# FoX attention and RWKV-7 in one stream of matmuls: transposes and logits set at other distances

## The chip, the core and the metric

One core of a Trainium2 chip runs the kernel in one launch. TensorE (PE in the profile) does the matmuls, VectorE (DVE), ScalarE (ACT) and GpSimd (POOL) the elementwise work, SyncE (SP) issues most transfers. The metric is the time of one execution on the device in microseconds (us), the median of several runs.

## The reference

A decoder layer in fp32 on 512 tokens of width 2048. One input projection feeds two mixers with 16 heads of 64 each:

```
z = rmsnorm(x) @ w_in                     # RWKV columns, FoX columns, gates
RWKV-7, per head, token by token:
  S = S * w - (S kk) (kk a)^T + v k^T ;  y = S r      # then group norm, bonus, SiLU gate
FoX, per head, in blocks of 128 queries:
  logits = q k^T / 8 + c_q - c_k          # c: running sum of log forget gates; causal
  o = softmax(logits) v                   # then SiLU gate
merged = sigmoid(g1) * (y_rw @ w_up_rwkv) + sigmoid(g2) * (y_fox @ w_up_fox)
x = x + merged @ w_out ; x = x + (p @ ple_proj) * sigmoid(rmsnorm(x) @ ple_gate_w) ; rmsnorm
```

## The kernel before

Every large product is done as three matmuls of 128x512 (high times high, high times low, low times high part of an fp32 number; `step`, L157). ScalarE makes the high part `hi` and VectorE the low part `lo` of each weight slab (L155, L156), a few slabs ahead. The instructions of a product stand in the main stream of TensorE; a block of 16 steps, 48 matmuls, makes one 128x512 result.

The mixers work on pairs of heads. For each of eight pairs `p` the main stream does the RWKV products k, v, r, g (`rw_k` ...) and then the FoX products k, q, v, g (`fx_k` ...), and seven blocks of gate products follow the last pair. Beside it two generators run per pair, `rw_mixer` and `fox_mixer`. Each does a little work and then yields a number of nanoseconds: the time, counted by the model in `Tensor.t` from the start of that piece of work, before which it is not called again. `Streams.drive` takes a generator's next piece when its time has come and otherwise the next step of the main stream. So the order on TensorE is fixed when the program is built, by these numbers; at run time TensorE takes its instructions strictly in that order and waits where one isn't ready. The order on the other engines is the framework's, except where `keep` pins it.

`fox_mixer` goes over eight blocks of a pair, four per head. `decays` prepares the bias of a block on GpSimd (`dd`, two buffers). `weights` does the logits in two matmuls (`lg`), which VectorE reads while adding the bias (L753, tile `dd`, with the row minimum `nm`); ScalarE does the exponential and the scaling. Later the weights are transposed by TensorE (`pT`, one transpose per 128 columns), ScalarE copies them out (`pt`, L789), and `values` multiplies them with the values (`po`) one block later. `lg`, `pT` and the transposed values `fvt` all use one PSUM bank (tag `F`, one buffer, L705): each must wait until the one before has been read. Before the change a round is: `lg` of block b+1, 5200 ns, `pT` of block b, and `lg` of block b+2 1500 ns after that.

`rw_mixer` works in PSUM tiles of tag `A`, two buffers that all its tiles take in turn: among others `gb` and `gk` (products of the decayed keys; VectorE reads them at L542, L543, L562, L564), `bo` and `rv`, the inverse in `x3` and `x4`, `u` (which ScalarE copies into `bd`, L632), `tr`, `py`, and at the end the transposes `yt` of the pair before (read by ScalarE, L694). L552 and L565 are the two yields that the diff touches, ahead of `gk` and ahead of `bo` and `rv`.

Of the kernel before, what the change touches and what calls it, by code (L numbers as in the profile page):

```python
# [108 lines left out]
def build(tc, a, out, dbg=None):  # L109
# [300 lines left out]
    def psa(shape, name):  # L410
        return psx.tile(shape, F32, tag="A", bufs=2, name=name)
# [4 lines left out]
    def need(z, *names):  # L416
        while any(n not in z for n in names):
            yield 450

    def rw_mixer(p, z):  # L420
# [128 lines left out]
            dma.dma_start(ldr[i : i + 8].rearrange("c i t -> i c t"), lt[bs, :, 32 * b : 32 * b + 32])  # L549
        lr = b4([P, 32, 32], f"lr{p}")  # L550
        dma.dma_start(lr, ldr.unsqueeze(0).to_broadcast([4, 32, 32, 32]).rearrange("g q i t -> g q (i t)"))
        yield 3500  # L552
        both = []
        for q in range(2):
            ps = psa([P, 4, P], f"gk{p}_{q}")
# [3 lines left out]
        for q, ps in enumerate(both):  # L559
# [2 lines left out]
                v.tensor_tensor(lak[half(h), cs, half(h)], ps[half(h), :, 0:64],  # L562
                                smb(slice(0, 64), half(h)), op=ALU.mult)
            v.tensor_tensor(ka[:, cs, 0:64], ps[:, :, 64:128], smb(slice(64, 128), slice(0, P)), op=ALU.mult)  # L564
        yield 5000  # L565
        ps = psa([P, T], f"bo{p}")
        pe.matmul(ps, bonesr, rh, start=True, stop=False)
        pe.matmul(ps, bonesr, rl, start=False, stop=True)
# [131 lines left out]
    def f2(name, bufs=None):  # L700
        return big.tile([P, T], F32, tag="f2", bufs=F2, name=name)

    def psf(shape, name):
        return psx.tile(shape, F32, tag="F", bufs=1, name=name)

    def fox_mixer(p, z):
        vt = f2(f"fvt{p}").rearrange("p (j d) -> p j d", d=P)
        done = []

        def token_major():  # L710
            ps = psf([P, 4, P], f"fvt{p}")
            for j in range(4):
                pe.transpose(ps[:, j], z["v"][:, j * P : (j + 1) * P], ident)
            s.copy(vt, ps)
            done.append(1)

        yield from need(z, "k", "q")
        q, k = z["q"], z["k"]

        qs, ks = ([big.tile([P, T], F32R, tag="f2", bufs=F2, name=f"{n}{p}_{h}") for h in range(2)] for n in ("qs", "ks"))  # L720
        kl = [small["kl", h] for h in range(2)]
        for h in range(2):
            hs, ho = slice(64 * h, 64 * h + 64), slice(64 - 64 * h, 128 - 64 * h)
            s.copy(qs[h][hs], q[hs])
            v.tensor_tensor(qs[h][ho], q[hs], qs[h][hs].bitcast(F32), op=ALU.subtract)
            s.copy(ks[h][hs], k[hs])
            s.copy(ks[h][ho], k[hs])
            v.tensor_tensor(kl[h][hs], k[hs], ks[h][hs].bitcast(F32), op=ALU.subtract)
            yield 1400
        o = f2(f"fo{p}")  # L730
        blocks = [(h, i) for h in range(2) for i in range(4)]
        cb, dds, pos = {}, {}, {}

        def fetch(h):
            cb[h] = big.tile([P, T], F32, tag="cb", bufs=1, name=f"cb{2 * p + h}")
            dma.dma_start(cb[h], cdr[2 * p + h : 2 * p + h + 1, :].to_broadcast([P, T]))

        def decays(h, i):

            hd, n = 2 * p + h, (i + 1) * P  # L740
            dd = dds[h, i] = big.tile([P, T], F32, tag="dd", bufs=2, name=f"dd{hd}_{i}")
            g.tensor_scalar(dd[:, :n], cb[h][:, :n], -1.0, cq[:, i, hd : hd + 1], op0=ALU.mult, op1=ALU.add)  # L742
            g.affine_select(out=dd[:, n - P : n], in_=dd[:, n - P : n], pattern=[[-1, P]], compare_op=ALU.is_ge,
                            fill=NEG, base=0, channel_multiplier=1)

        def weights(h, i):
            hd, n, dd = 2 * p + h, (i + 1) * P, dds[h, i]
            nm = big.tile([P, 2], F32, tag="nm", bufs=4, name=f"nm{hd}_{i}")
            lg = psf([P, T], f"lg{hd}_{i}")
            pe.matmul(lg[:, :n], qs[h][:, i * P : n], ks[h][:, 0:n], start=True, stop=False)  # L750
            pe.matmul(lg[:, :n], qs[h][:, i * P : n], kl[h][:, 0:n], start=False, stop=True)

            v.tensor_tensor_reduce(dd[:, :n], lg[:, :n], dd[:, :n], -1.0, 3.4e38, op0=ALU.add, op1=ALU.min,  # L753
                                   accum_out=nm[:, 0:1])
            s.activation(dd[:, :n], dd[:, :n], AF.Exp, scale=-1.0, bias=nm[:, 0:1], accum_out=nm[:, 1:2])  # L755
            v.reciprocal(nm[:, 1:2], nm[:, 1:2])
            s.activation(dd[:, :n], dd[:, :n], AF.Copy, scale=nm[:, 1:2])

        def values(h, i, pt):

            hs = slice(64 * h, 64 * h + 64)
            if i == 0:
                pos[h] = psx.tile([P, T], F32, tag="O", bufs=1, name=f"po{p}_{h}")
            for j in range(i + 1):
                pe.matmul(pos[h][:, i * P : (i + 1) * P], vt[:, j], pt[:, j], start=(j == 0), stop=(j == i))
            if i == 3:
                s.copy(o[hs], pos[h][hs])

        late = []

        fetch(0)
        yield 4000
        decays(0, 0)
        yield 1500
        weights(0, 0)
        for b, (h, i) in enumerate(blocks):
            if (h, i) == (0, 3):
                fetch(1)
                yield 4000
            if b < 7:  # L780
                decays(*blocks[b + 1])
                yield 1500
                weights(*blocks[b + 1])
            yield 5200 if b < 7 else 5500
            ps = psf([P, 4, P], f"pT{2 * p + h}_{i}")
            for j in range(i + 1):
                pe.transpose(ps[:, j], dds[h, i][:, j * P : (j + 1) * P], ident)
            pt = big.tile([P, 4, P], F32, tag="pt", bufs=2, name=f"pt{2 * p + h}_{i}")
            s.copy(pt[:, 0 : i + 1], ps[:, 0 : i + 1])  # L789
            if late:  # L790
                late.pop()()
            late.append(lambda h=h, i=i, pt=pt: values(h, i, pt))
            if not done:
                yield 2200
                yield from need(z, "v")
                yield 1500
                token_major()
                yield 1300
        yield 2600
        late.pop()()  # L800
        yield from need(z, "g")
        sg = f2(f"fsg{p}")
        s.activation(sg, z["g"], AF.Tanh)
        v.scalar_tensor_tensor(sg, sg, 1.0, z["g"], op0=ALU.add, op1=ALU.mult)
        y = f2(f"fy{p}")
        v.tensor_tensor(y, o, sg, op=ALU.mult)
        dma.dma_start(ydr_fx[p], y)
# [9 lines left out]
    def main():  # L817
# [15 lines left out]
        for p in range(NPAIR):  # L833
            z = {}
            streams.spawn(rw_mixer(p, z))
            for name, i in RW_ORDER:
                if (p, i) == (0, RW_ORDER[0][1]):
                    ps = small["ps_r"]
                else:
                    ps = psmain(f"rw{p}_{name}")  # L840
                    yield from product(ps, w_rw[p, i], xs)
                zt = b2(f"z{name}{p}")
                shifted(big, ps, 8 * i + p, zt)
                z[name] = zt
            z = {}
            streams.spawn(fox_mixer(p, z))
            for name, i in FX_ORDER:
                ps = psmain(f"fx{p}_{name}")
                yield from product(ps, w_fx[p, i], xs)
                zt = f2(f"fz{name}{p}")  # L850
                if name in "qg":
                    v.scalar_tensor_tensor(zt, ps, 0.125 if name == "q" else 0.5, rb, op0=ALU.mult, op1=ALU.mult)
                else:
                    v.tensor_tensor(zt, ps, rb, op=ALU.mult)
                z[name] = zt
# [283 lines left out]
```

## Time and profile before

| | |
|---|---|
| median of 3 runs | 1925.48 us (1923.34 to 1926.66) |
| the profiled execution | 1926.43 us, span 1924.7 us |
| TensorE busy in it | 1885.3 us, 98% of the span |
| VectorE, ScalarE, GpSimd busy | 1044.9, 853.3, 160.3 us |
| granted TensorE clock, mean | 0.994 of full speed |

The span goes from the first to the last instruction; 1.73 us of the execution lie outside it. The mixers run from about 40 to 1060 us, the gates and up-projections to 1535, the output projection to 1709, the rest to the end. A wait is shown at the instruction that waited, with the instruction that released it. A matmul's shown length includes its way through the array, so that matmuls overlap in the rows: the distance from start to start is what one costs.

### The profile page before, as it was taken

How to read it: one execution, taken by the hardware profiler on the slowest of the kernel's cores; microseconds unless marked ns; L12 is line 12 of the kernel's file. 1: busy time of each engine (PE TensorE's matmuls, PEld its weight loads, DVE VectorE, ACT ScalarE, POOL GpSimd, SP SyncE). 2: the span in 40 equal slices, each digit the busy share in tenths (PEclk: the TensorE clock that was granted, in tenths of full speed). 3: DMA queues.
4: the chain of work that ended last, by engine and by line, in shares of the span. 5: the costliest groups of instructions: out<-in, count | busy, mean ns of one | idle time of the engine just before them, and what ended most of it. 6: DMA issues, size and time to landing. Idle time of an engine off the chain costs nothing.

```text
span 1924.7 us, 26112 instructions
## 1 busy us (share of the span) xinstructions
PE 1885.3 (98%) x9722; PEld 1573.5 (82%) x9722; DVE 1044.9 (54%) x2255; ACT 853.3 (44%) x1608; POOL 160.3 (8%) x281
## 2 busy tenths in 40 slices
PE   8999999999999999999999999999999999999997
PEld 6878888888888888888888888888888888888887
DVE  7765756757567576675754433343333533434445
ACT  6536346364563644636446322232222433334333
POOL 1201102011020110201101000000000001101112
PEclk9999999999999999999999999999999999999998
DMA  5331322323222222232323533342233344463224
GB/s 169 94 93 64 107 80 86 95 72 99 88 78 100 76 96 88 74 102 64 106 89 98 181 115 110 99 140 92 97 99 99 99 142 141 155 207 99 96 95 161
DMA packets 87391, 204.31 MB, mean 106 GB/s; under 512 B 24784, under 2 KB 31184, under 8 KB 87264
## 3 DMA queue, kind: packets, MB, share of 16 engines
q1 hardware_dynamic: 85888, 201.39, 32.7%
q8 instruction: 76, 1.25, 0.3%
q10 hardware_dynamic: 1376, 1.25, 0.2%
q14 instruction: 51, 0.42, 0.1%
HBM read 186.06 MB, written 16.55 MB: 105 GB/s over the span
## 4 chain that ended last, share of the span: by engine, by line
PE 52%; ACT 1%; DVE 1%; issue 0%; POOL 0%; DVEq 0%
PE gate L63 18%; PE pg L63 9%; PE up L63 9%; PE wo L63 9%; PE pp L63 1%; PE rw_g L63 1%; PE fx_q L63 1%; PE fx_k L63 1%; PE py L63 0%; PE fx_g L63 0%; PE po L63 0%; PE rw_r L63 0%; PE lg L63 0%; ACT bd L632 0%; PE rw_v L63 0%
## 5 line engine op out<-in xcount | busy, mean ns | idle before, releaser
L155 ACT CAST hi<-raw 128x512 fp32r<-128x512 f32 x595 | 368.7, 621 | 796.9 <-PE gate L63 211.5
L156 DVE TENSOR_TENSOR lo<-raw,hi 128x512 fp32r<-128x512 f32 x596 | 412.8, 694 | 483.5 <-ACT hi L155 466.5
L63 PE MATMUL gate<-xh,hi 128*128 128x512 f32 x512 | 201.0, 393 | 0.0
L63 PE MATMUL gate<-xh,lo 128*128 128x512 f32 x512 | 199.6, 390 | 0.0
L63 PE MATMUL gate<-xl,hi 128*128 128x512 f32 x512 | 199.5, 390 | 0.0
L63 PEld LDWEIGHTS gate<-xh,lo 128*128 128x128 f32 x512 | 96.1, 188 | 20.1
L63 PEld LDWEIGHTS gate<-xh,hi 128*128 128x128 f32 x512 | 96.2, 188 | 19.3
L63 PEld LDWEIGHTS gate<-xl,hi 128*128 128x128 f32 x512 | 96.2, 188 | 19.3
L63 PE MATMUL pg<-x2h,hi 128*128 128x512 f32 (+1 forms) x304 | 109.0, 359 | 0.0
L63 PE MATMUL pg<-x2h,lo 128*128 128x512 f32 (+1 forms) x304 | 108.3, 356 | 0.0
L63 PE MATMUL pg<-x2l,hi 128*128 128x512 f32 (+1 forms) x304 | 108.2, 356 | 0.0
L742 POOL TENSOR_SCALAR dd<-cb,cq 128x128 f32<-128x128 f32 (+1 forms) x64 | 39.8, 622 | 663.0 <-PE pT L70 602.2
L595 DVE TENSOR_TENSOR nn<-nn,tp 128x240 f32<-128x240 f32 (+14 forms) x240 | 69.1, 288 | 7.3
L935 POOL TENSOR_TENSOR acc<-acc,sq 128x512 f32<-128x512 f32 x15 | 19.4, 1291 | 643.6 <-ACT sq L934 643.6
L591 DVE TENSOR_TENSOR tp<-nn,lr 128x240 f32<-128x240 f32 (+14 forms) x240 | 68.7, 286 | 5.9
L63 PEld LDWEIGHTS pg<-x2h,hi 128*128 128x128 f32 x304 | 57.5, 189 | 8.8 <-ACT hi L155 0.5
L63 PEld LDWEIGHTS pg<-x2h,lo 128*128 128x128 f32 x304 | 57.5, 189 | 8.5 <-DVE lo L156 0.4
L63 PEld LDWEIGHTS pg<-x2l,hi 128*128 128x128 f32 x304 | 57.5, 189 | 8.3 <-issue 0.2
L63 PE MATMUL rw_g<-xh,hi 128*128 128x512 f32 x128 | 53.5, 418 | 0.0
L63 PE MATMUL rw_r<-xh,hi 128*128 128x512 f32 x128 | 53.2, 415 | 0.0
L63 PE MATMUL rw_v<-xh,hi 128*128 128x512 f32 x128 | 53.0, 414 | 0.0
L755 ACT ACTIVATE dd<-dd,nm 128x128 f32<-128x128 f32 (+1 forms) x64 | 35.9, 562 | 37.4 <-DVE nm L753 36.9
(544 smaller groups left out, 4411.8 us busy)
## 6 DMA issues: line engine op xcount, KB each, us to landing
raw<-in_w_mix SPq DMA_DIRECT2D x126, 512.0 KB
raw<-in_w_gate SPq DMA_DIRECT2D x64, 512.0 KB
raw<-in_w_pg SPq DMA_DIRECT2D x36, 512.0 KB
raw<-in_w_out SPq DMA_DIRECT2D x32, 512.0 KB
raw<-in_w_up_rw SPq DMA_DIRECT2D x16, 512.0 KB
raw<-in_w_up_fox SPq DMA_DIRECT2D x16, 512.0 KB
x<-in_xT SPq DMA_DIRECT2D x16, 256.0 KB
cb<-cdr SPq DMA_DIRECT2D x16, 256.0 KB
```

Source lines behind the costliest of these rows:

```text
L63: self.eng.matmul(out, lhsT, rhs, start=start, stop=stop, skip_group_check=skip)
L155: (v.tensor_copy if made[0] == 0 else s.copy)(hi[:, :w], src)
L156: v.tensor_tensor(lo[:, :w], src, hi[:, :w].bitcast(F32), op=ALU.subtract)
L591: one = v.tensor_tensor(tp[:, :, 0:m], nn[:, :, j : j + 1].to_broadcast([P, 8, m]), lr[:, j : j + 1, j + 1 : 32].to_broadcast([P, 8, m]), ...
L595: v.tensor_tensor(nn[:, :, j + 1 : 32], nn[:, :, j + 1 : 32], tp[:, :, 0:m], op=ALU.add)
L742: g.tensor_scalar(dd[:, :n], cb[h][:, :n], -1.0, cq[:, i, hd : hd + 1], op0=ALU.mult, op1=ALU.add)
L755: s.activation(dd[:, :n], dd[:, :n], AF.Exp, scale=-1.0, bias=nm[:, 0:1], accum_out=nm[:, 1:2])
L935: g.tensor_tensor(acc, acc, sq, op=ALU.add)
```

## The change

In `fox_mixer` the yield of 5200 ns between the logits of block b+1 and the transposes of block b becomes 2600 ns, and 2600 ns are added between the transposes and the next piece (for all blocks; for block 0 in place of 2200 ns, and after the last block in place of the 2600 ns that stood behind the loop). After the logits of block 0 there are 4000 ns more before those of block 1. In `rw_mixer` the yield before `gk` grows from 3500 to 4400 ns, the one before `bo` and `rv` from 5000 to 6000 ns. No operation is added or removed; the moves are in the order of instructions.

```diff
@@ rw_mixer
-        yield 3500
+        yield 4400
         both = []
         for q in range(2):
             ps = psa([P, 4, P], f"gk{p}_{q}")
...
-        yield 5000
+        yield 6000
         ps = psa([P, T], f"bo{p}")
@@ fox_mixer
         weights(0, 0)
+        yield 4000
         for b, (h, i) in enumerate(blocks):
...
                 weights(*blocks[b + 1])
-            yield 5200 if b < 7 else 5500
+            yield 2600 if b < 7 else 5500
             ps = psf([P, 4, P], f"pT{2 * p + h}_{i}")
...
             late.append(lambda h=h, i=i, pt=pt: values(h, i, pt))
+            yield 2600
             if not done:
-                yield 2200
                 yield from need(z, "v")
                 yield 1500
                 token_major()
                 yield 1300
-        yield 2600
         late.pop()()
```

Three places show what becomes of it, each from TensorE's order. The first is the opening of pair 3 during its last FoX product `fx3_g`: `lg6_0` and `lg6_1` are the logits of blocks 0 and 1 of head 6, `pT6_0` the transpose of block 0. Before:

```order
L63 MATMUL lg6_0_4796<-ks3_0_4680,qs3_0_4678 128x128
L63 MATMUL lg6_0_4796<-kl0_543,qs3_0_4678 128x128
L63 MATMUL fx3_g_4787<-xh1_206,hi128_4707 128x512
...
L63 MATMUL fx3_g_4787<-xh2_223,lo128_4708 128x512
L63 MATMUL lg6_1_4825<-ks3_0_4680,qs3_0_4678 128x256
L63 MATMUL lg6_1_4825<-kl0_543,qs3_0_4678 128x256
L63 MATMUL fx3_g_4787<-xh3_232,hi128_4707 128x512
...
L70 MATMUL pT6_0_4866<-ident_71,dd6_0_4770 128x128
```

Of the same place, the changed kernel's order:

```order
L63 MATMUL lg6_0_4796<-ks3_0_4680,qs3_0_4678 128x128
L63 MATMUL lg6_0_4796<-kl0_543,qs3_0_4678 128x128
L63 MATMUL fx3_g_4787<-xh1_206,hi128_4707 128x512
...
L63 MATMUL lg6_1_4856<-ks3_0_4680,qs3_0_4678 128x256
L63 MATMUL lg6_1_4856<-kl0_543,qs3_0_4678 128x256
L63 MATMUL fx3_g_4787<-xh10_353,hi130_4756 128x512
...
L63 MATMUL fx3_g_4787<-xh13_408,lo131_4789 128x512
L70 MATMUL pT6_0_4881<-ident_71,dd6_0_4770 128x128
```

Between the two logits stood 6 matmuls of the product, now 27; from the second logits to the transpose 24, now 12. Pair 0 has the same counts.

The second place is in the next RWKV product of the main stream, `rw4_k`: `u3`, `tr3` and `py3` belong to the RWKV mixer of pair 3, `pT6_1` are the transposes of block 1, `lg6_3` the logits of block 3. Before:

```order
L63 MATMUL u3_0_5014<-av3_4057,bd3_537 128x128 x4
L63 MATMUL u3_1_5019<-av3_4057,bd3_537 128x128 x4
...
L70 MATMUL pT6_1_5042<-ident_71,dd6_1_4803 128x128 x2
L63 MATMUL po3_0_5047<-pt6_0_4868,fvt3_4496 128x128
...
L63 MATMUL lg6_3_5061<-ks3_0_4680,qs3_0_4678 128x512
L63 MATMUL lg6_3_5061<-kl0_543,qs3_0_4678 128x512
L63 MATMUL tr3_0_5069<-ba3_4058,bd0_531 128x128 x3
```

And in the changed kernel:

```order
L63 MATMUL u3_0_5021<-av3_4044,bd3_537 128x128 x4
L63 MATMUL u3_1_5026<-av3_4044,bd3_537 128x128 x4
L70 MATMUL pT6_1_5039<-ident_71,dd6_1_4837 128x128 x2
L63 MATMUL po3_0_5044<-pt6_0_4883,fvt3_4485 128x128
...
L63 MATMUL tr3_0_5070<-ba3_4045,bd0_531 128x128 x3
...
L63 MATMUL tr3_1_5085<-ba3_4045,bd0_531 128x128 x4
...
L63 MATMUL lg6_3_5102<-ks3_0_4680,qs3_0_4678 128x512
L63 MATMUL lg6_3_5102<-kl0_543,qs3_0_4678 128x512
```

The logits `lg6_3` stood 6 product matmuls behind the transposes and ahead of `tr3`; now they stand behind both `tr3` and all sixteen `py3` rows, and the transposes come right after `u3`, with 12 product matmuls between them and `tr3` (before, 6 on either side of the transposes, and the logits).

The third place is at the end of `rw4_g`, where the RWKV mixers of pairs 3 and 4 meet: `gb4`, `gk4`, `bo4`, `rv4` of pair 4 and `yt3` of pair 3. Before:

```order
L63 MATMUL gk4_0_5567<-ar4_5150,bd1_533 128x128 x4
L63 MATMUL gk4_1_5572<-ar4_5150,bd1_533 128x128 x4
...
L70 MATMUL yt3_5603<-ident_71,yc3_5441 128x128 x4
L63 MATMUL bo4_5613<-rkh4_5483,bonesr_94 128x512
L63 MATMUL bo4_5613<-rkl4_5484,bonesr_94 128x512
L63 MATMUL rv4_5618<-vst4_5371,bd2_535 128x64 x8
```

In the changed kernel, with the logits and transposes of head 7 that now stand there:

```order
L63 MATMUL lg7_3_5509<-kl1_547,qs3_1_4679 128x512
L63 MATMUL gb4_0_5517<-ar4_5147,bd0_531 128x128 x4
L63 MATMUL gb4_1_5522<-ar4_5147,bd0_531 128x128 x4
...
L70 MATMUL pT7_2_5542<-ident_71,dd7_2_5389 128x128 x3
...
L63 MATMUL gk4_1_5565<-ar4_5147,bd1_533 128x128 x4
...
L70 MATMUL yt3_5579<-ident_71,yc3_5421 128x128 x4
...
L63 MATMUL bo4_5610<-rkh4_5470,bonesr_94 128x512
L63 MATMUL bo4_5610<-rkl4_5471,bonesr_94 128x512
L63 MATMUL rv4_5615<-vst4_5352,bd2_535 128x64 x8
```

`yt3` comes 3 product matmuls behind `gk4_1` (before, 9 and four `po`), and 15 product matmuls stand between `yt3` and `bo4`, where there was none. `pT7_2` stands 3 product matmuls and the eight `gb4` behind its preceding logits `lg7_3`.

## Rows read from the trace of the kernel before

**Rows 1.** Page, part 1: engine, busy us (share of the span), instructions.
```profile
PE 1885.3 (98%) x9722; PEld 1573.5 (82%) x9722; DVE 1044.9 (54%) x2255; ACT 853.3 (44%) x1608; POOL 160.3 (8%) x281
```

**Rows 2.** Waits of TensorE: waiter <- releaser: us in total, times, longest us.
```profile
PE lg L63 <- ACT pt L789: 9.8, 14, 1.2
PE lg L63 <- DVE nm L753: 4.3, 8, 2.8
...
PE rv L63 <- ACT yt L694: 2.4, 6, 0.4
...
PE gk L63 <- DVE ba L543: 1.2, 2, 0.8
```

**Rows 3.** Windows: stretch us, its length, busy time (count) per engine, granted clock, DMA.
```profile
126.90:137.00 10.10, 7.33 (x22) 5.55 (x21) 7.14 (x32) 2.82 (x8) 0.00 (x0) 0.66 0.15 56
...
500.00:980.00 480.00, 471.36 (x2724) 395.79 (x2722) 314.32 (x778) 252.65 (x513) 50.34 (x94) 1.00 0.27 87
...
1110.00:1900.00 790.00, 789.97 (x3588) 657.98 (x3587) 320.42 (x489) 268.71 (x447) 40.41 (x42) 1.00 0.37 119
```

**Rows 4.** Timeline of TensorE, opening block of pair 0: start us, us, idle before.
```profile
126.76 0.39 PE L63 MATMUL fx_g<-xl,hi 128*128 128x512 f32 x1
126.99 0.39 PE L63 MATMUL fx_g<-xh,lo 128*128 128x512 f32 x1
130.15 0.58 PE L63 MATMUL lg<-ks,qs 128*128 128x256 f32 x1 [2.77 <-DVE nm L753]
...
130.74 0.63 PE L63 MATMUL fx_g<-xh,hi 128*128 128x512 f32 x1
...
136.27 0.40 PE L63 MATMUL fx_g<-xl,hi 128*128 128x512 f32 x1
```

**Rows 5.** Timeline of VectorE, the same stretch.
```profile
129.80 0.28 DVE L753 CUSTOM_DVE_ANT_0 dd<-lg,dd 128x128 f32<-128x128 f32 x1
```

**Rows 6.** Timeline of TensorE, one pair (heads 12 and 13).
```profile
860.92 0.39 PE L63 MATMUL lg<-ks,qs 128*128 128x256 f32 x1 [0.21 <-DVE nm L753]
...
861.26 0.40 PE L63 MATMUL fx_g<-xh,hi 128*128 128x512 f32 x1
...
885.58 0.50 PE L63 MATMUL lg<-ks,qs 128*128 128x512 f32 x1 [0.81 <-ACT pt L789]
...
906.71 0.39 PE L63 MATMUL lg<-ks,qs 128*128 128x256 f32 x1 [0.60 <-ACT pt L789]
...
907.05 0.39 PE L63 MATMUL rw_v<-xh,hi 128*128 128x512 f32 x1
...
922.18 0.39 PE L63 MATMUL rw_r<-xh,lo 128*128 128x512 f32 x1
922.62 0.50 PE L63 MATMUL lg<-ks,qs 128*128 128x512 f32 x1
...
942.25 2.00 PE L63 MATMUL rv<-vst,bd 128*128 128x64 f32 x16 [0.40 <-ACT yt L694]
```

**Rows 7.** Tile pT: who waited for it (us, times).
```profile
  PEld lg L63: 18.0, 21
```

**Rows 8.** Timeline of VectorE, the latest reading of logits in a pair.
```profile
908.90 0.42 DVE L753 CUSTOM_DVE_ANT_0 dd<-lg,dd 128x256 f32<-128x256 f32 x1
```

**Rows 9.** Timeline of ScalarE after the `u` matmuls of the same pair.
```profile
880.56 0.36 ACT L632 COPY bd<-u 64x256 f32<-64x256 f32 x1 [0.21 <-PE u L63]
...
881.85 0.37 ACT L632 COPY bd<-u 64x256 f32<-64x256 f32 x1
...
882.87 2.26 ACT L632 COPY bd<-u 64x256 f32<-64x256 f32 x6
```

**Rows 10.** Timeline of TensorE, `gk` of the next pair.
```profile
936.04 1.95 PE L63 MATMUL gk<-ar,bd 128*128 128x128 f32 x16
937.83 0.39 PE L63 MATMUL po<-pt,fvt 128*128 128x128 f32 x2
```

**Rows 11.** Timeline of VectorE, the last reading of the first `gk` bank.
```profile
938.00 0.42 DVE L564 TENSOR_TENSOR ka<-gk,sm 128x256 f32<-128x256 f32 x1
```

## The prediction, made before the changed kernel ran

> **What bounds the kernel now.** I read the page's busy times first: TensorE is busy for 98% of the span [rows 1], and the chain of waits that ended last runs along it. What TensorE doesn't do is therefore time of the kernel, and a microsecond of waiting taken from it is a microsecond won, unless it waits somewhere else instead. The windows say where it waits [rows 3]: from 500 to 980 us, four pairs of heads in full mixing, it is idle for 480.00 - 471.36 = 8.64 us, 2.2 us a pair; from 1110 to 1900 us it is idle for 0.03 us. So there is nothing to win outside the mixers. The list of TensorE's waits names the places [rows 2]: logits wait for the copy of the transposes before them in their bank, 9.8 us in 14 waits; logits wait for VectorE to have read the logits before them, 4.3 us in 8; `rv` waits for ScalarE to read `yt`, 2.4 us in 6; `gk` waits for VectorE to read `gb`, 1.2 us in 2. The four come to 17.7 us, and the diff moves exactly these.
>
> A stop costs more than the idle time shown. A product matmul is shown as 0.39 us long, but the next starts 0.23 us after it (126.76 to 126.99) [rows 4]: after a stop the overlap of 0.16 us is lost too. It also happens without any idle time in TensorE's rows: the logits at 922.62 start 0.44 us after the matmul ahead of them, 0.21 late [rows 6]. The weight loads show these as well: 21 of them waited for the copy of transposes, 7 more than the 14 [rows 7].
>
> **The change part by part.**
>
> *Opening block later (4000 ns).* In pair 0 the second logits wait 2.77 us, and what follows runs slow: the granted clock of that stretch is 0.66, that is part of it at 1.2 instead of 2.4 GHz, after TensorE had stood still [rows 3, 4]. From 126.99 to 136.27 us TensorE does one product matmul, two logits and 13 product matmuls in 9.28 us. At full clock these take 0.23 + 0.34 + 13 x 0.23 = 3.56 us (0.34 is 860.92 to 861.26, the same logits in a later pair [rows 6]). Lost: 5.7 us. With 27 product matmuls ahead of the second logits instead of 6 they come 21 x 0.23 = 4.8 us later, at 132 us, and VectorE reads the first ones at 129.80 [rows 5]. The stop goes and, as no idle time precedes them, the slow matmuls with it. In the other seven pairs the same wait is 4.3 - 2.77 = 1.5 us in all, with 7 x 0.16 for the restarts 2.6 us; a reading that is late by 0.21 us [rows 6] is in time with 4.8 us more.
>
> *Transposes away from the next logits.* From a transpose to the logits after it there were 1500 ns, now 4100 ns, counted from the start of the transposes. The 14 waits and their restarts are 9.8 + 14 x 0.16 = 12.0 us, the 7 small ones 7 x 0.21 = 1.5 us: 13.5 us. The longest idle time in this class in a pair is 0.81 us [rows 6], so 2600 ns more clear all of them, also where ScalarE is behind by twice as much.
>
> *The two RWKV parts.* `rv` needs the bank of `yt` and stood two `bo` matmuls behind it; now 15 product matmuls are between, 3.4 us more than the 0.40 us waited [rows 6]. Six waits: 2.4 + 6 x 0.16 = 3.4 us. `gk` waited in pair 1 alone, 1.2 + 2 x 0.16 = 1.5 us; in the new order it stands 15 product matmuls behind `gb` there instead of 3, three `pT`, `po` and 3, so this goes too.
>
> Sum of what goes: 5.7 + 2.6 + 13.5 + 3.4 + 1.5 = 26.7 us.
>
> *What is late next.* First, the transposes. They stood 4.8 us or more behind the logits whose bank they take; in the new order 2.5 to 2.9 us (12 product matmuls, or 3 and eight `gb` of 0.22). VectorE must have read the logits by then. Its latest reading within a pair is of logits whose last start is 906.94 and whose follower starts at 907.05: it ends at 908.90 + 0.42 = 909.32 [rows 6, 8], 2.3 us behind. So the latest case fits with 0.2 us to spare, and others are earlier; but VectorE's order changes too, and in each pair `pT` behind `lg` and `gb` at 2.5 us meets VectorE's busiest stretch, the end of the r chain. I put 0 to 0.5 us there per pair and take 0.15. In pair 0 VectorE is still at the inverse when the second logits come; this transpose may wait 0 to 2 us, I take 0.3. Second, `yt`. It takes the bank of the first `gk`, 3 product matmuls and the second `gk` behind it: 0.68 + 0.90 = 1.58 us. The 16 half matmuls of `gk` go from 936.04 to 937.83, so the first bank is issued by 936.94, and its last reading ends at 938.00 + 0.42 = 938.42 [rows 10, 11], 1.48 us later. That fits by 0.1 us; I take 0.1 a pair with the restart, of 0 to 0.5. Third, `u` still waits for VectorE a little, as before. In all 7 x 0.25 + 0.3 = 2 us come back (0 at best, 7 x 1.0 + 2 = 9 at worst).
>
> Net 26.7 - 2 = 24.7 us. The chain of a block from logits to transposes gets 2.6 us shorter for the softmax, which hides it: before, transposes stood 7 us or more behind their own logits, in the new order 9 us or more. The rounds get longer by the rounding of two yields instead of one, so a pair's last transposes slide into the next pair's `fx_k`; its output is read only by the up-projections behind the mixers. SP issues the same transfers in nearly the same order.
>
> On the clock, the windows say that from 500 to 980 us it is granted in full, 1.00, in spite of about five stops a pair of up to 0.81 us [rows 3, 6]. The Trainium skill says otherwise of such a pattern (page "TensorE: Matmul & The Clock Gate", section "A second HAM failure mode: psum-queue depth-cycling"): when TensorE idles briefly between groups because it cycles through PSUM, the clock goes down and up between bursts. By that rule each of the 30 or so stops would cost as the first did, 13 x 0.20 = 2.6 us more, and the change would win another 75 us; the row excludes it for stops of this length, so it gets none of the chance, and I count the slow matmuls once.
>
> **The rivals.**
>
> *The wait moves to `tr`.* While the logits waited for ScalarE (885.58), ScalarE was busy with eight copies out of `u`, 0.37 us each, the last six from 882.87 in 2.26 us [rows 9]. `tr` needs the same copies and stood behind these logits. In the new order nothing waits ahead of it, and it comes 3.2 us after `u` (12 x 0.23, and two `pT` and a `po` at 0.11 a half matmul as in [rows 10]). If it now waits instead, 6 x (0.81 + 0.16) = 5.8 us come back: 1901.7 + 5.8 = 1907.5. Against it: its first matmuls need only the first two copies, at 880.56 and 881.85, 1.3 us apart, and the last copies are needed by `py` 3 us later. 12%.
>
> *Other meetings take half of it.* The streams are timed by the model's clock, and the changed order shifts `pn`, `at`, `bt`, `kt`, `vt` and the copies on ScalarE by up to 1 us, and the old order shows how easily such a place stops. New stops of about 2 us a pair, seven times, make 14 us: 1916. For it: the stops of a pair [rows 6] repeat in the next, so one bad meeting costs six times. Against it: I found none under 1.1 us distance that was not there before. 10%.
>
> *Slower: transposes wait in place of logits.* Place: `pT`, bank F, 56 times (all but each pair's last block). Price: what VectorE's reading exceeds 2.7 us by, plus 0.16. For the 24.7 us to be lost it must exceed by 0.28 us on average, a reading 3 us behind the logits every time; the latest seen in a pair is 2.3 us. At 3.2 us it is 56 x 0.66 = 37 us: 1926.4 - 26.7 + 37 = 1937. The trace has one reading that late, in pair 0 [rows 5], where the inverse filled VectorE. 4%. The Trainium skill has a rule on this side (page "Perfetto Trace Analysis", section "Optimizing Tensor Performance"): independent groups should rotate through different PSUM banks, so that the emptying of one lies beside the matmuls of the next. The change keeps one bank, and by the rule alone the wait would only change its place; the trace agrees that the wait exists but shows it gone wherever 5 us lie between.
>
> *The opening wait stays*, since VectorE, not the distance, is late: pair 0 keeps its 5.7 us, 1907. It reads at 129.80, two microseconds ahead of the new place. 4%.
>
> **How the numbers follow.** The sums are on the profiled execution: 1926.4 - 24.7 = 1901.7 us, which is 0.95 above the median of the runs shown, 1925.5. I predict 1901. Chances: forecast 70%, with a range of its own of 1898 (nothing comes back, and the rest of `u`) to 1908 (all comes back that I bounded); `tr` 12%; other meetings 10%; slower 4%; opening 4%. The range 1897 to 1913 leaves out the worse half of the other meetings and the slow case, and a little below. What a measurement of this kernel can't tell from no change is 0.2%, 3.9 us: faster needs less than 1921.6. That gives 94% faster, 3% the same (parts of the other meetings and the slow side at its threshold), 3% slower.
>
> **What would show it.** In the changed profile the waits of logits for `pt` and for `nm` and of `rv` for `yt` are gone from TensorE's list, the idle time from 500 to 980 us falls from 8.64 to under 3 us, the stretch around 130 us is at full clock, and the pairs are about 3 us closer to each other. Wrong would be the appearance of `pT` or `tr` in that list with more than 1 us a pair, or a stretch of low clock that isn't there now. If the waits go as said and the time doesn't, my first step (that all of TensorE's idle time is time of the kernel) is wrong.

## The result and the profile after

The changed kernel takes 1893.9 us (median of four runs, 1892.2 to 1895.7) against 1926.1 for the one before, run beside it (1923.3 to 1927.0): ratio 0.9835, 95% interval 0.9818 to 0.9852. The forecast was 1901 us, with a range from 1897 to 1913. The direction was right and the four kinds of stop that it named went, but the gain was some 7 us larger, more than the range allowed. The profiled execution took 1895.7 us, span 1894.0.

TensorE's waits of the changed kernel (waiter <- releaser: us in total, times, longest), whole but for the start and the end of the program; it answers to [rows 2]:

```profile
PE pcr L70 <- ACT ka L502: 1.6, 1, 1.6
PE pg L63 <- ACT hi L155: 1.3, 1, 1.3
...
PE u L63 <- issue: 0.2, 1, 0.2
```

Logits, `rv` and `gk` are gone from it, and neither `pT` nor `tr` came in. The windows answer to [rows 3] (stretch, length, busy us and count of PE, PEld, DVE, ACT, POOL, granted clock, DMA share, GB/s):

```profile
126.90:137.00 10.10, 10.10 (x48) 8.32 (x47) 8.32 (x33) 4.33 (x11) 0.90 (x2) 1.00 0.33 109
500.00:980.00 480.00, 479.55 (x2814) 408.48 (x2813) 319.51 (x799) 254.78 (x528) 49.29 (x96) 1.00 0.29 89
```

The stretch around 130 us is at full clock. From 500 to 980 us TensorE is idle for 0.45 us instead of 8.64. It runs 2814 instructions there instead of 2724. Over the whole span [rows 1] has 1885.3 us busy, the page after 1871.6: of the 30.7 us that the span lost, 17.0 were shown as idle and 13.7 as busy time.

The opening of pair 0 on TensorE's timeline (start, duration), for [rows 4]; the next fence is VectorE's reading of the first logits, for [rows 5]:

```profile
124.63 0.28 PE L63 MATMUL lg<-kl,qs 128*128 128x128 f32 x1
...
130.93 0.28 PE L63 MATMUL lg<-ks,qs 128*128 128x256 f32 x1
131.04 0.28 PE L63 MATMUL lg<-kl,qs 128*128 128x256 f32 x1
131.16 0.40 PE L63 MATMUL fx_g<-xh,hi 128*128 128x512 f32 x1
```

```profile
127.11 0.28 DVE L753 CUSTOM_DVE_ANT_0 dd<-lg,dd 128x128 f32<-128x128 f32 x1
```

The second logits come 6.3 us behind the first, and VectorE has read those 3.5 us earlier. TensorE's timeline at the two places in a pair that the prediction dealt with last (`yt` and `rv`), and at one that it didn't name (`kt`):

```profile
757.12 0.62 PE L70 MATMUL bt<-ident,kr 128*128 128x128 f32 x4
757.87 0.66 PE L70 MATMUL kt<-ident,kp 128*128 128x128 f32 x4
...
789.75 0.63 PE L70 MATMUL yt<-ident,yc 128*128 128x128 f32 x4
790.14 0.48 PE L63 MATMUL rw_g<-xh,hi 128*128 128x512 f32 x1
...
793.66 0.39 PE L63 MATMUL bo<-rkh,bonesr 128*128 128x512 f32 x1
793.90 0.40 PE L63 MATMUL bo<-rkl,bonesr 128*128 128x512 f32 x1
794.13 1.89 PE L63 MATMUL rv<-vst,bd 128*128 128x64 f32 x16
```

`yt` stands 15 product matmuls ahead of `bo`, and `rv` starts 0.23 us behind `bo`'s second, where it had an idle time of 0.40 us ahead of it [rows 6]. `kt` is a new small stop: it starts 0.75 us behind `bt`, whose four transposes take 0.11 us each.

**What was lost where.** For every matmul of TensorE's timeline I took the time to the start of the next one, less what it streams at full clock (0.227 us for 512 columns, in proportion for fewer), and summed what exceeds 0.06 us, from pair 0's `fx_k` to the first gate product. The row "all else" depends on what is counted for the shortest matmuls (in strict proportion it is about 31 and 30); the rows above it hardly do:

```
us lost                                     before   after
logits stopped by pt                         13.7      0
logits stopped by nm                          5.6      0
rv, gk stopped                                5.0      0
13 products at half clock behind 130 us       2.7      0
second matmul behind lg, rv, gk; bo           5.8     2.4
u, its stop and the slow u behind it          4.2     1.5
kt, bt, lo, yt, pT, py                        0.9     5.2
all else (switches between streams)          15.5    14.6
sum                                          53.3    23.7
```

By its rows the sum falls by 29.7 us. By the starts themselves the same stretch is 30.7 us shorter; 1 us lies in losses below 0.06.

### The profile page after: what moved, and what is told of

The parts are those of the page before. It is cut to its first block, busy times and chain, and to the rows that moved or that the text cites. A ratio compares the mean times of both kernels' runs of the same rounds, so it can differ in the third digit from the quotient of the medians.

```text
span 1894.0 us, 26139 instructions
## 1 busy us (share of the span) xinstructions
PE 1871.6 (99%) x9722; PEld 1570.5 (83%) x9722; DVE 1044.3 (55%) x2255; ACT 847.7 (45%) x1608; POOL 157.2 (8%) x281
## 3 DMA queue, kind: packets, MB, share of 16 engines
q8 instruction: 76, 1.25, 0.3%
q10 hardware_dynamic: 1376, 1.25, 0.2%
## 4 chain that ended last, share of the span: by engine, by line
PE 90%; ACT 3%; DVE 2%; DMA 1%; issue 0%; POOL 0%; DVEq 0%; SPq 0%; ACTq 0%
PE gate L63 18%; PE wo L63 9%; PE up L63 9%; PE pg L63 9%; PE fx_g L63 5%; PE fx_k L63 5%; PE fx_q L63 5%; PE fx_v L63 5%; PE rw_g L63 4%; PE rw_r L63 4%; PE rw_k L63 3%; PE py L63 2%; PE po L63 2%; PE rw_v L63 2%; PE lg L63 1%; PE pp L63 1%
## 5 line engine op out<-in xcount | busy, mean ns | idle before, releaser
L742 POOL TENSOR_SCALAR dd<-cb,cq 128x128 f32<-128x128 f32 (+1 forms) x64 | 40.2, 629 | 737.7 <-PE pT L70 596.8
```

## The experiments

Each kernel is described by its edit. "Net" is the shift of the first gate product between the traces, less the shift that was already there at pair 0's `fx_k`: the start of the program differs from execution to execution (last section).

**Pair 0's opening alone.**

```
         weights(0, 0)
+        if p == 0:
+            yield 4000
```

> The kernel before with the opening's 4000 ns in pair 0 alone. Theory A (the stop and the slow matmuls behind it are the price, as the prediction has it): the 2.77 us stop of the second logits goes, the stretch from 126 to 137 us is at full clock, and every pair from 1 on starts 5.7 to 5.9 us earlier; the later pairs keep their stops and their period of 121.3 us; 1926 - 6 = 1920 us. Rival (VectorE is late whatever the distance, the stop returns at the transposes behind): 2 us or less.

1916.4 us, ratio 0.9968 (0.9954 to 0.9982); net -7.1 us: 6.0 by the next pair's start, 1.6 more in pair 1, and 0.5 given back after. The waits:

```profile
PE lg L63 <- ACT pt L791: 9.8, 14, 1.2
PE rv L63 <- ACT yt L694: 2.4, 6, 0.4
...
PE lg L63 <- DVE nm L753: 1.5, 7, 0.2
```

Eight waits for `nm` became seven of 0.2 us: theory A, within 0.3 us of its 5.7. The 1.6 us of pair 1, which the expectation didn't have, are its two `gk` waits: they are gone from the list too, though `gk` stands as close behind `gb` as before.

**The transposes alone.**

```
-            yield 5200 if b < 7 else 5500
+            yield 2600 if b < 7 else 5500
...
             late.append(lambda h=h, i=i, pt=pt: values(h, i, pt))
+            yield 2600
             if not done:
-                yield 2200
...
-        yield 2600
         late.pop()()
```

> The kernel before with only the transposes moved (2600 ns on either side). In this order yt stands 12 product matmuls ahead of bo, so the stop of rv should go with those of the logits, without the RWKV edit; u stands as close behind its solve as before, so its stop of 0.15 us stays, and the openings keep their stop. Theory A (a stop costs its idle time and 0.16 us): logits 13.5 + rv 3.4 = 17 us, 1909. Theory B (a stop also makes the second matmul behind it start 0.1 us late, and a switch from product to small work costs 0.09 us): logits 15.7 + rv 4.6 = 20 us, 1906. Slower rival (the transposes wait instead): over 1915, with pT in the list of waits.

1907.2 us, ratio 0.9915 (0.9900 to 0.9929); net -15.1 us. The waits:

```profile
PE lg L63 <- DVE nm L753: 4.9, 8, 3.0
...
PE py L63 <- DVE st L659: 1.5, 6, 0.3
PE gb L63 <- DVE ar L523: 1.4, 6, 0.2
```

The logits are free of `pt` and `rv` of `yt`, as expected, but `py` and `gb` have six stops each that no theory had, 7.1 us with what follows them by the account above. This is what the prediction called other meetings, here for an order in which only one edit was made. `u` was expected to keep its stop; it loses 2.1 us instead of 4.2, in an order that has nothing new between the solve and `u`.

**The two RWKV parts alone** (4400 and 6000, all else as before).

> The kernel before with only the two RWKV parts later (4400 and 6000 ns). Stops of rv (six) and of gk (pair 1) go, all others stay, u's among them. Theory A (idle time and 0.16 us each): 3.4 + 1.5 = 4.9 us, 1921. Theory B (with the second matmul and the slow bo pair in front): 4.6 + 1.8 = 6.4 us, 1919.5; the period of pairs 2 to 6 falls by 0.57 (A) or 0.76 us (B).

1912.0 us, ratio 0.9939 (0.9924 to 0.9954); net -11.5 us, about twice what either theory said. From pair 2 on the period falls by 0.58 us, as in A. The rest lies ahead: 4.6 us in pair 0 and 3.3 in pair 1. In pair 1 the `gk` stops account for 1.8 us, and the rest is mainly one stop of logits by `pt`, the longest of before (1.25 us), which is gone. For pair 0 the waits, the window of the opening, and the first logits on TensorE with their reading on VectorE show why:

```profile
PE lg L63 <- ACT pt L789: 8.5, 13, 0.8
PE lg L63 <- DVE nm L753: 2.5, 8, 1.0
```

```profile
124.00:136.00 12.00, 11.05 (x52) 9.07 (x52) 8.72 (x33) 4.57 (x11) 0.92 (x2) 1.00 0.30 100
```

```profile
122.31 0.22 PE L63 MATMUL lg<-ks,qs 128*128 128x128 f32 x1
124.66 0.28 DVE L753 CUSTOM_DVE_ANT_0 dd<-lg,dd 128x128 f32<-128x128 f32 x1
```

With the inverse later by the two yields, VectorE gets to pair 0's first logits earlier: it starts to read them 2.4 us behind their first matmul, where it took 4.2 before (125.62 to 129.80, [rows 5]). The stop is 0.95 instead of 2.77 us and no slow matmuls follow it. So the opening stop has two causes, the logits' distance and VectorE's queue, and either edit removes most of it.

**`u` 600 ns later, in the kernel before.**

```
-        yield 2000
+        yield 2600
         bua, buv = bdb, bdk
...
-        yield 4600
+        yield 4000
```

> The kernel before with u 600 ns later and the part behind it left at its place: three product matmuls more ahead of u in pairs 1 to 7, no other instruction of TensorE moved. Theory A (the prediction: u's small wait isn't worth counting): the time stays within 1 us, or what u gains comes back at tr, which has 600 ns less. Theory B (u's stop is part of what the change removed, by lg between the solve and u): 0.5 us a pair, 3 us in all, 1923, and the pair's period falls from 121.3 to 120.8 us.

1925.3 us, ratio 1.0004 (0.9994 to 1.0013). `u` has no stop left, and nothing is won. TensorE's list, its timeline in pair 4, and ScalarE's in the same stretch:

```profile
PE lg L63 <- ACT pt L789: 14.6, 15, 1.5
```

```profile
756.70 0.38 PE L63 MATMUL u<-av,bd 128*128 128x128 f32 x2
...
762.63 0.50 PE L63 MATMUL lg<-ks,qs 128*128 128x512 f32 x1 [1.47 <-ACT pt L789]
```

```profile
759.54 2.64 ACT L632 COPY bd<-u 64x256 f32<-64x256 f32 x7
762.20 0.37 ACT L789 COPY pt<-pT 128x256 f32<-128x256 f32 x1
```

The copy of the transposes stands on ScalarE behind the eight copies out of `u`, and the logits wait for that copy. They start 5.9 us after `u`, nearly as before (764.31 - 758.13 = 6.2). So theory A holds as to the time, but what `u` gained came back at the logits and not at `tr`. The three products put ahead of `u` are the three that lay between `u` and the transposes: the logits' stop grew from 0.79 to 1.47 us. (The Trainium skill, page "PSUM — Partial Sum Buffer", section "Engine vs sequencer instructions", has ScalarE's queue as strictly first in, first out; these rows agree.)

**`u` 600 ns earlier, in the changed kernel** (1400 and 5200), the counterpart:

> The changed kernel with u 600 ns earlier and the part behind it left at its place: from pair 2 on three product matmuls move from ahead of u to behind it, so that u comes 0.80 us behind the end of its solve's last matmuls, against 1.48 in the changed kernel and 1.13 in the one before, where it waited 0.15. Pair 1 is shuffled as well. Theory A (in the new order nothing behind u absorbs its stop, so u's 2.7 us were a real part of the gain): u waits about 0.5 us, 0.9 with what follows, the period rises from 117.7 to about 118.6 us, 6 us in all: 1900. Theory B (a stop of u is absorbed behind it, as e4_u's gain was): u in the list of waits but the time within 1.5 us of the changed kernel, 1894.

1896.5 us, ratio 0.9861 (0.9841 to 0.9882); net -26.8 us against -30.7 of the changed kernel: 3.8 us come back, all of them at `u`, 0.6 us a pair. (The medians differ by 2.6 us and the intervals of the two ratios overlap, so the price rests on the traces.)

```profile
PE u L63 <- PE lo L63: 3.5, 6, 0.6
```

Nothing behind absorbs it: in the new order the logits behind `u` stand 10 us after it, and their bank has long been copied. It is theory A, with a smaller price than its 0.9 us a pair.

**The changed kernel without the opening's 4000 ns.**

> The changed kernel without the opening's 4000 ns. Theory A (each part has its own price): the stops of the opening logits come back, 5.9 us in pair 0 and 2.7 us in the others, 1902.5. Theory B (the 4000 ns move the whole attention of a pair against the RWKV stream, and that is what clears u and keeps py and gb from the stops they had with the transposes alone): these come back as well, u 0.4 us, py 0.55 and gb 0.5 us a pair, and yt stands right behind gk, 1911 or more.

1909.3 us, ratio 0.9922 (0.9907 to 0.9937). Of the 32 us 15 are gone: far from theory A, and within 2 us of theory B.

```profile
PE yt L70 <- DVE ka L564: 3.5, 6, 0.6
PE lg L63 <- DVE nm L753: 2.8, 8, 1.2
...
PE py L63 <- DVE st L659: 1.5, 6, 0.3
PE gb L63 <- DVE ar L523: 1.3, 6, 0.2
```

By the account above only 4.1 us are the opening logits; `py` and `gb` lose 7.1, `yt` 5.3 and `u` 2.1 (1.5 in the changed kernel). `yt` stands right behind `gk` and takes the bank whose reading the prediction had worked out as 1.5 us behind.

**The changed kernel without the two RWKV edits** (3500 and 5000).

> The changed kernel without the two RWKV edits. Theory A (the RWKV edit is what removes the stops of rv and gk): 5 us come back, 1899, with rv in the list of waits. Theory B (in the new order yt already stands nine product matmuls ahead of bo, so rv has no stop to lose): within 1 us of the changed kernel, 1894, no rv in the list; gk, 0.7 us nearer to gb, may wait up to 0.2 us a pair.

1894.2 us, ratio 0.9841 (0.9826 to 0.9856): theory B. Net -29.7 us, so the two edits are worth 1.0 us in the whole, though 11.5 by themselves; no `rv` and no `gk` wait, and what comes back are three stops of pair 0's mixers, between 133 and 148 us:

```profile
PE x L63 <- ACT x L611: 1.2, 2, 0.8
PE pT L70 <- DVE nm L753: 0.6, 1, 0.6
```

**The transposes nearer to the logits ahead of them** (1300 and 3900 in the changed kernel).

> The changed kernel with the transposes 1300 ns behind the logits that they follow in their bank and 3900 ns ahead of the next, in place of 2600 and 2600. In a pair they then stand 0.8 to 1.6 us behind logits instead of 2.4 to 2.9. If VectorE's reading of the logits needs 1.3 to 2.3 us, as in the trace of before, the transposes wait 0.3 to 1 us with their restart, some six times a pair: 15 to 40 us, 1909 to 1934, pT heading the list of waits. If the reading is shorter and the 2600 ns were not needed: 1894, no pT in the list.

1918.7 us, ratio 0.9972 (0.9960 to 0.9985): 25 us slower than the changed kernel.

```profile
PE pT L70 <- DVE nm L753: 15.4, 15, 2.2
...
PE yt L70 <- DVE ka L564: 1.8, 3, 0.6
```

The slower rival's mechanism is real, and 1300 ns from the place that was chosen. Its shape was other than I had it: not a little at each of 56 transposes but one to three stops a pair, 0.2 to 2.2 us long and one of them over 1.2 in every pair, where VectorE is late. One of the longest, with the logits, their reading and the transposes that waited for it:

```profile
306.04 0.34 PE L63 MATMUL lg<-kl,qs 128*128 128x384 f32 x1
309.32 0.55 DVE L753 CUSTOM_DVE_ANT_0 dd<-lg,dd 128x384 f32<-128x384 f32 x1
309.94 0.44 PE L70 MATMUL pT<-ident,dd 128*128 128x128 f32 x2 [2.18 <-DVE nm L753]
```

The reading ends 3.8 us behind the start of the second logits matmul; in the changed kernel, apart from pair 0's first logits, none ends later than 2.2 us behind it.

**The two stops that are left in the mixers.**

```
-        yield 2400
+        yield 5000
         pcr = psx.tile([16, T], F32, tag="A", bufs=2, name="pcr")
...
-        yield 6000 if p == 0 else 3600
+        yield 6000 if p == 0 else 4500
         ps = token_major("bt", lambda j: kr[:, j * P : (j + 1) * P])
```

> The changed kernel with the two stops taken away that it still has in the mixers: bt 900 ns later in pairs 1 to 7 (six product matmuls more between at and bt), pcr 2600 ns later. Theory (a stop removed is time won when nothing new is late): kt 2.0 us and the slow bt ahead 0.4 us, pcr 1.6 us of idle time and 5 slow matmuls of 0.2 us behind it, 5 us in all: 1889. Rival (these stops only move, as others did): 1893 to 1895.

1887.4 us, ratio 0.9807 (0.9792 to 0.9822): the fastest version, 6 us under the changed kernel. Its windows at `pcr` and in the mixers:

```profile
78.20:81.60 3.40, 3.40 (x20) 2.90 (x19) 1.32 (x3) 3.29 (x8) 0.00 (x0) 1.00 0.18 60
500.00:980.00 480.00, 480.00 (x2808) 409.00 (x2807) 320.25 (x800) 255.06 (x524) 48.67 (x96) 1.00 0.28 89
```

TensorE has no idle time in this stretch any more. Of the difference to the changed kernel's trace 3.1 us lie at `pcr` and 1.6 in the pairs: the theory, not the rival.

## Why the prediction was too small

Two steps made the forecast too small: the price of a stop, and the step that took `u` to be unchanged.

*That TensorE's waiting is the kernel's time*: right. The four targeted stops and the slow matmuls were put at 26.7 us; the table has 13.7 + 5.6 + 5.0 + 2.7 = 27.0.

*The price of a stop*, idle time and 0.16 us: mis-sized, for it counts one matmul. The one behind is late as well, by 0.09 to 0.13 us: the second of the logits, the second `rv` and `gk`, and `bo` ahead of `rv`. That makes 5.8 - 2.4 = 3.4 us that the sum didn't have. The trace of before showed it: 860.92 to 861.26 in [rows 6], which the prediction took as the full-clock length of two 256-column logits, 0.34 us, was such a case. In the changed kernel the same two take 0.23 (130.93 to 131.16).

*"`u` still waits a little, as before"*: this step was wrong. The new order puts the next logits between the solve (the `x` matmuls) and `u`, so that 1.48 us of matmuls at full rate stand between them instead of 1.13, and 2.7 us of `u`'s 4.2 go. The logits are not shown to be the only cause: with the transposes alone 2.1 us went without them, and what else made `u` ready sooner there wasn't traced. That the 2.7 us count in the new order and would not have counted in the old one is what the two `u` experiments show: 3.8 us lost in the one, 0 gained in the other.

*"What is late next"*, 2 us at `pT` and `yt`: too small, and at the wrong places. `pT` and `yt` lose 0.7 us; `kt` (2.6 with its second matmul, 0.9 before), `lo` 1.1 and `bt` 0.5 take the most. In all 4.3 us come back.

The balance: 24.7 + 0.3 + 3.4 + 2.7 + 0.9 (other switches) + 1.0 (below 0.06 us) - 2.3 (more came back than the 2 us said) = 30.7 us, the shift in the trace. Two misses outside the sum nearly cancel: the start was 1.0 us shorter in this execution, and `pg` once waited 1.3 us at 1688.75 us. The range reached down by 4 us only, for the rest of `u` and for nothing coming back; it held no room for a price that was too low at some forty stops at once.

*The opening*: 5.7 us were said, and 5.9 measured in pair 0 with the change, 6.0 alone. But the reason was incomplete: the RWKV yields take most of it as well, and the 4000 ns are worth 15 us in the whole, not 8.3, since they set where the attention stands against the RWKV stream in every pair. *`rv` and `gk`*: the stops go by the RWKV edits alone, but in the whole they would have gone without them: `yt` has already moved away, and `gk` is free with pair 0's opening alone.

*The rivals*: `tr` never waited. Other meetings cost 7 us with the transposes alone, and in the full change 4.3. The slower case is shown by the transposes at 1300 ns. The clock: what the Trainium skill tells of short idle stretches between groups (page "TensorE: Matmul & The Clock Gate", section "A second HAM failure mode: psum-queue depth-cycling"), a clock that goes down and up again with them, wasn't seen at the stops of the mixers up to 1.47 us; six of that length, a pair apart, left it at 1.00 (last section).

What stays open: bank rotation wasn't tried, what set VectorE's order at 1300 ns wasn't traced, and why `u` was ready sooner with the transposes alone isn't known.

## What to carry to other kernels

In a stream that is full, a wait is removed by work that must come from somewhere: products put ahead of one stop are taken from ahead of another, so count the whole loop, and every place where two instructions changed their order, before calling a small wait unchanged. Price a stop by the starts of the matmuls around it until they are back at their full-rate distance, not by the idle time. Edits that shift one stream against another do not add up (7.1 us for the opening of pair 0, 15.1 and 11.5 alone, 30.7 for the whole, and one of them worth 1.0 in the end): test the whole, then take parts away.

## What the runs showed of the hardware

**Stops and the clock.** The window of the kernel with `u` later, around its `nm` stop of 2.84 us, and around one of its six stops of 1.47 us:

```profile
125.30:133.00 7.70, 4.86 (x16) 3.89 (x16) 6.54 (x30) 2.53 (x7) 0.00 (x0) 0.78 0.18 68
760.00:767.00 7.00, 5.53 (x43) 4.89 (x42) 2.37 (x7) 4.86 (x12) 0.73 (x2) 1.00 0.12 42
```

Behind the long one six products start 0.43 us apart (the 1.2 GHz level), then 0.23; behind the short ones the clock is not touched. The kernel before had 13 such products behind 2.77 us, that with the transposes alone 5, and one half as late, behind 3.02 us: about the same stop costs 1.1 to 2.6 us of slow matmuls from one execution to the other.

The length of a stop doesn't decide it alone. The stop of `pcr` is 1.59 us long in ten of the eleven traces; in nine of them a stretch at half clock stands there, as in the changed kernel's (first line), but not in the trace with the transposes at 1300 ns (second line). In that trace the stop of 2.18 us at 309.94 us leaves the clock at 1.00 too (third line):

```profile
77.50:81.00 3.50, 3.40 (x12) 2.63 (x13) 1.11 (x2) 0.05 (x1) 0.00 (x0) 0.57 0.44 153
76.00:84.00 8.00, 8.00 (x46) 6.84 (x45) 3.31 (x5) 5.09 (x10) 0.72 (x1) 1.00 0.27 80
306.00:314.00 8.00, 5.82 (x36) 4.86 (x35) 7.19 (x17) 3.88 (x8) 3.17 (x5) 1.00 0.30 91
```

**The start.** Pair 0's `rw_v` starts at 43.73 us in the profiled execution before, and 0 to 3.5 us earlier in those of the other kernels, whose code up to there is the same. The first `ssq` waits 1.0 to 2.6 us, and the clock goes with it: in the five traces where it waits 2.1 us or more a stretch at half clock stands behind or beside the wait and `rw_v` starts at 41.5 to 43.8 us, in the six where it waits 1.0 to 1.6 us the clock stays full there and `rw_v` starts at 40.2 to 41.0. The same stretch before, and with pair 0's opening alone:

```profile
31.00:38.00 7.00, 4.36 (x11) 2.58 (x11) 4.56 (x8) 4.62 (x7) 0.00 (x0) 0.76 0.41 143
31.00:38.00 7.00, 6.17 (x25) 4.33 (x26) 4.27 (x8) 3.78 (x4) 0.00 (x0) 1.00 0.22 76
```

A microsecond between two kernels is read from shifts behind that point, not from medians alone.
